# A 16-batch matmul with bias and residual on one core: joint waits and a joint store in SyncE's program, and the last store in two transfers by partitions

## The chip, the cores and the metric

The kernel runs on one core of one Trainium2 chip. The metric is device time in microseconds; the changed kernel is timed against the kernel before on the same chip. Before: 211.24 us, the median of three runs (211.44, 210.61, 211.24). The profile shows one execution more, of 211.06 us, whose span from the first to the last instruction is 208.7 us.

A core has a matrix engine (PE, its weight loads shown as PEld), VectorE (DVE), ScalarE (ACT), GpSimd (POOL) and SyncE (SP). Each follows its own list of instructions and waits on semaphores. Data moves between the large memory and the 128 partitions of the core's own memory through 16 transfer (DMA) engines. Here SP alone issues transfers.

## The reference

```python
def reference(x, weight, bias, residual):      # x: 16 x 512 x 1024, weight: 1024 x 768, all fp32
    return (np.matmul(x, weight) + bias + residual).astype(np.float32)
```

Flattened, x has 8,192 rows of 1,024 numbers; the residual and the output have 8,192 rows of 768.

## The kernel before

**Tiling.** The 8,192 rows form 8 groups of 1,024. In a group each of the 128 partitions holds 8 rows that follow one another in memory, so one group of x is 32 KB for each partition, one group of the residual or the output 24 KB. A row index j = 0 to 7 over all partitions is a subtile; there are 64 of them (`n_sub`).

**Buffers.** One large tensor `data` holds four places for residual groups (`r_home`, L97) and two for x groups (`x_half`, L94). Group g's residual lies in place g % 4, but that of group 7 (the last) lies in an x place. The weight is first loaded, as fp32, into residual place 3. Output is made in place: residual + product + bias, and is stored from there. So every load waits until what lay in its place has been used.

**Compute.** For each half of a group, ACT casts x to bf16 (`cast_x`, L112: two casts for a half, four for a group, each adding 1 to the semaphore `cast`), DVE and ACT transpose it in blocks, PE multiplies it by the weight into PSUM, DVE adds the product onto the residual (`evacuate`, L146, semaphore `ev`), and POOL adds the bias to two subtiles at a time (`add_bias`, L188, semaphore `add`). POOL also casts the weight at the start (L182, semaphore `wc`, which ends at `R` = 8). The last two subtiles get their bias ahead of the product, so for them DVE's `evacuate` comes last.

**SyncE's program.** The list `ORDER` (L16) names all transfers in the order in which SP issues them, and the loop at L216 makes waits and a transfer of each name:

- `x2a` is the first half (rows 0 to 3) of group 2's x, `x2b` the second. From group 2 on, part a waits until the first half of group g-2 has been cast, part b until both have (L227).
- `r3` is group 3's residual. It waits for `wc`, because the weight lay in its place; r7 waits for casts, r4 to r6 wait for a store from their place (L233 to L238).
- `load_into` (L208) makes a load wait for the one before it on the same semaphore: x parts a on `xa`, parts b on `xb`, residuals on `r`. So SP issues each next load of a kind only when the one before it has landed.
- `st5` is group 5's store; it waits for POOL's adds of the group's last subtiles. The stores from st3 on count on one semaphore, `st`. The last group's store is in three, by rows: `st7a` (0 to 3), `st7b` (4 and 5), `st7c` (6 and 7). st7c waits for DVE's last evacuation.
- At the end, SP waits until all stores from st3 on have landed (L253).

SP takes its list strictly in order: while it waits for one entry, all later ones are held up. All transfers go through one hardware queue and are worked off in about the order of issue. A transfer can carry one wait in its own instruction; a second wait is an instruction of its own (shown with L73).

Of the kernel before, what the change touches and what calls it, by code (L numbers as in the profile page):

```python
# [10 lines left out]
P = 128  # L11
Q = 32
G = 8
B = 4

ORDER = ("x0a w0 w1 bias x0b r0 x1a x1b r1 x2a x2b r2 x3a x3b r3 x4a x4b st0 st1 r4 x5a x5b r5 "  # L16
         "st2 x6a x6b r6 x7a x7b r7 st3 st4 st5 st6 st7a st7b st7c ").split()
PARTS = {"": (0, 8), "a": (0, 4), "b": (4, 8)}
LAST_PARTS = {"a": (0, 4), "b": (4, 6), "c": (6, 8)}


@with_exitstack
def kernel(
    ctx: ExitStack,
    tc: tile.TileContext,
    x: bass.AP,
    weight: bass.AP,
    bias: bass.AP,
    residual: bass.AP,
    out: bass.AP,  # L30
):
    nc = tc.nc
    with tc.tile_critical(name="all", no_gpsimd_drain=True), ExitStack() as es:  # L33
        emit(nc, es, x, weight, bias, residual, out)


def emit(nc, es, x, weight, bias, residual, out):
    x2d = x.flatten_outer_dims()
    res2d = residual.flatten_outer_dims()
    out2d = out.flatten_outer_dims()  # L40
    M, K = x2d.shape
    N = weight.shape[1]
    R = K // P
    KH = K // 2
    n_sub = M // P
    n_grp = n_sub // G
    n_bat = n_sub // B
    chunks = [(0, 512), (512, N - 512)]
    sp, act, dve, pool, pe = nc.sync, nc.scalar, nc.vector, nc.gpsimd, nc.tensor
# [4 lines left out]
    R_SLOT, X_SLOT = G * N, G * K  # L54
# [12 lines left out]
    def sem(name):  # L67
        if name not in sems:
            sems[name] = es.enter_context(nc.semaphore(name))
        return sems[name]  # L70

    def wait(eng, name, value):
        eng.wait_ge(sem(name), value)  # L73
# [14 lines left out]
    def group(ap, g):  # L88
        return ap[g * G * P:(g + 1) * G * P, :].rearrange("(p j) k -> p j k", p=P)

    def span(start, size):
        return data[:, start:start + size] if isinstance(start, int) else data[:, bass.ds(start, size)]

    def x_half(g, half):  # L94
        return span(X0 - (g % 2) * X_SLOT + half * (B * K), B * K).rearrange("p (t k) -> p t k", k=K)

    def r_home(g):  # L97

        return (g % 4) * R_SLOT + ((g + 1) // n_grp) * (X0 - 3 * R_SLOT)

    def r_rows(start, j, n):
        return span(start + j * N, n * N).rearrange("p (j n) -> p j n", n=N)
# [51 lines left out]
    cast, pt, res = Rising(dve, "cast", 1, 1), Rising(dve, "pt", 2, 2), Rising(dve, "r", 16, 16)  # L154
# [51 lines left out]
    landed, stored = {}, 0  # L206

    def load_into(name):  # L208

        before = landed.get(name, 0)  # L210
        landed[name] = before + 16
        if before:
            wait(sp, name, before)
        return name

    for name in ORDER:  # L216
        into = name
        if name == "bias":
            wait(sp, "ev", EV0)
            src, dst = bias[None, :].to_broadcast((P // Q, N)), bias_rows[0:P:Q, :]  # L220
        elif name[0] == "w":
            k0 = int(name[1]) * (R // 2)
            src, dst = w_rows[:, k0:k0 + R // 2, :], w_stage[:, k0:k0 + R // 2, :]
        elif name[0] == "x":
            g, part = int(name[1]), name[2:]
            j0, j1 = PARTS[part]
            if g > 1:  # L227
                wait(sp, "cast", 2 * (2 * g - 2 - (part == "a")))
            into = load_into(name[0] + part)
            src, dst = group(x2d, g)[:, j0:j1, :], x_half(g, j0 // B)  # L230
        elif name[0] == "r":
            g = int(name[1])
            if g == 3:  # L233
                wait(sp, "wc", R)
            elif g == n_grp - 1:
                wait(sp, "cast", 2 * (2 * g))
            elif g > 3:
                wait(sp, f"st{g - 4}", 16)  # L238
            into = load_into("r")
            src, dst = group(res2d, g), r_rows(r_home(g), 0, G)  # L240
        else:
            g = int(name[2])
            j0, j1 = (LAST_PARTS if g == n_grp - 1 else PARTS)[name[3:]]
            end = g * G + j1
            if end == n_sub:
                wait(sp, "ev", ev_end)
            else:
                wait(sp, "add", added[end - 1])
            src, dst = r_rows(r_home(g), j0, j1 - j0), group(out2d, g)[:, j0:j1, :]
            if g > 2:  # L250
                into, stored = "st", stored + 16
        sp.dma_start(out=dst, in_=src).then_inc(sem(into), 16)
    wait(sp, "st", stored)  # L253

# [2 lines left out]
    with pe.Fori(0, n_bat) as b:  # L257
        mv.wait()
        tm.wait()
        for i in range(B):  # L260
# [4 lines left out]
            for k in range(R):  # L265
                lhsT = words[:, k // 2, k % 2, :]
                for c, (n0, nl) in enumerate(chunks):
                    dst, rhs = po[:, i, n0:n0 + nl], w_sb[:, k, n0:n0 + nl]
                    if c == 0:
                        ins = pe.matmul(dst, lhsT=lhsT, rhs=rhs, start=(k == 0), stop=(k == R - 1))  # L270
                    else:
                        ins = pe.add_instruction(mybir.InstMatmult(  # L272
                            name=nc.get_next_instruction_name(),
# [34 lines left out]
```

## Time and profile before

| | us |
|---|---|
| median of three runs | 211.24 |
| the profiled execution | 211.06 |
| its span, first to last instruction | 208.7 |
| PE busy | 170.1 |
| DVE busy | 166.4 |
| ACT busy | 154.0 |
| POOL busy | 116.3 |

The shares of the span are 82, 80, 74 and 56%. The transfers move 87.05 MB, 61.88 MB read and 25.17 MB written, 417 GB/s over the span. The transfers that bear on the change, with the time from the issue by SP to the landing of the data:

| transfers | count | KB each | median us to landing |
|---|---|---|---|
| x halves | 16 | 2,048 | 17.0 |
| residual groups | 8 | 3,072 | 17.1 |
| stores of a group | 7 | 3,072 | 24.3 |
| st7a | 1 | 1,536 | 10.1 |
| st7b, st7c | 2 | 768 | 8.6 |

A transfer that takes 17 us to land has spent most of that in the queue: 2,048 KB at 417 GB/s are 5.0 us.

How to read the profile: a row of digits shows 40 equal slices of the span, each digit the busy share of a slice in tenths. In a table of windows each row has a stretch of the span, its length, the busy time of five engines with their instructions in brackets, the granted clock of the matrix engine (1.00 is full), the busy share of the 16 transfer engines and the GB/s that they moved. In a timeline, a row has the start, the time covered, the engine, the line and the operation; where several instructions are merged the count stands at the end.

### The profile page before, as it was taken

The page shows a single profiled execution, that of the slowest core. Times are in us where ns is not written, and L with a number is a line of the kernel's source. Part 1 is how long each engine was busy: PE and PEld are TensorE (multiplying, and loading weights), DVE is VectorE, ACT ScalarE, POOL GpSimd, SP SyncE. Part 2 cuts the span into 40 slices and gives each one's busy share as a digit, 9 for nine tenths or more (in the row PEclk, how much of TensorE's full clock was granted, in tenths as well). Part 3 has the DMA queues.
Part 4 walks back from the last instruction along what each step waited for, and adds up shares of the span by engine and source line. Part 5 has one row for each costly group of instructions (what it writes and reads, how often), then busy time and mean ns, then how long its engine had stood idle before and what let it go on. Part 6 is the DMA issues. An engine that isn't in the chain of part 4 may idle for free.

```text
span 208.7 us, 2850 instructions
## 1 busy us (share of the span) xinstructions
PE 170.1 (82%) x1024; PEld 50.4 (24%) x512; DVE 166.4 (80%) x180; ACT 154.0 (74%) x168; POOL 116.3 (56%) x44
## 2 busy tenths in 40 slices
PE   0000499999999999999999999999999999999700
PEld 0000122232333233223322333232223332322200
DVE  1009686899989998999899989998999899983400
ACT  0365998697989798979997998889897989720000
POOL 0066003918484757566665757484839392999600
PEclk9999999999999999999999999999999999999965
DMA  6999899999999999999999999999999999999993
GB/s 226 426 434 465 386 430 446 451 407 421 433 437 418 468 386 446 433 448 405 429 448 407 459 410 433 419 433 437 422 426 451 429 415 438 443 424 424 422 418 135
DMA packets 5192, 87.05 MB, mean 417 GB/s; under 512 B 580, under 2 KB 580, under 8 KB 840
## 3 DMA queue, kind: packets, MB, share of 16 engines
q1 hardware_dynamic: 5192, 87.05, 97.8%
HBM read 61.88 MB, written 25.17 MB: 417 GB/s over the span
## 4 chain that ended last, share of the span: by engine, by line
DVE 30%; ACT 22%; issue 16%; DMA 15%; PE 10%; ACTq 1%; DVEq 1%; SPq 0%
DVE xt L142 17%; DMA data<-in_x_dram 15%; ACT xt L119 12%; ACT xb L114 8%; DVE tq L136 7%; PE po L270 7%; DVE data L148 6%; PE po L272 3%; ACT L114 2%; DVEq L84 1%; ACTq L84 0%; ACTq L114 0%; ACTq L124 0%; DVEq L148 0%; SPq L303 0%
## 5 line engine op out<-in xcount | busy, mean ns | idle before, releaser
L270 PE MATMUL po<-w_sb,xt 128*128 128x512 bf16 x512 | 169.2, 383 | 27.0 <-DVE xt L142 24.0
L190 POOL TENSOR_TENSOR data<-data,bias_bc 128x1536 f32<-128x1536 f32 x32 | 109.9, 3453 | 68.5 <-DVE data L148 68.5
L272 PE MATMUL po<-w_sb,xt 128*128 128x256 bf16 x512 | 140.7, 275 | 0.0
L119 ACT COPY xt<-tq 32x512 uint32<-32x512 uint32 x128 | 79.0, 617 | 20.1 <-DVE tq L136 17.4
L142 DVE STREAM_TRANSPOSE xt<-xb 32x512 uint32<-32x512 uint32 x128 | 90.1, 704 | 2.7 <-ACT xb L114 0.7
L270 PEld LDWEIGHTS po<-w_sb,xt 128*128 x512 | 50.4, 98 | 146.2 <-issue 144.2
L148 DVE TENSOR_TENSOR data<-po,data 128x1536 f32 (+2 forms) x33 | 56.0, 1709 | 12.3 <-PE po L272 11.8
L114 ACT CAST xb<-data 128x2048 bf16 x32 | 64.9, 2077 | 0.3
L136 DVE STREAM_TRANSPOSE tq<-xb 128x1024 uint32<-128x1024 uint32 x16 | 19.8, 1235 | 1.6 <-ACT xb L114 1.6
L114 ACT ACT_TABLE_LOAD x8 | 10.3, 1283 | 9.6 <-DMA data<-in_x_dram 9.5
L185 POOL CAST w_sb<-data 128x768 bf16<-128x768 f32 x8 | 6.3, 826 | 12.1 <-DMA data<-in_weight_dram 12.1
L153 DVE LOAD_MASK_SELECT bias_bc<-bias_rows x1 | 0.0, 14 | 13.9 <-DMA bias_rows<-in_bias_dram 13.9
L150 DVE MEMSET bias_rows<- 128x768 f32 x1 | 0.7, 698 | 1.2 <-SPq L33 1.2
L153 DVE STREAM_SHUFFLE bias_bc<-bias_rows 128x768 f32<-128x768 f32 x1 | 1.0, 1021 | 0.0
L292 POOL MEMSET const-float32-0.0<- 128x1 f32 x1 | 0.1, 98 | 0.2 <-issue 0.2
L292 POOL MEMSET const-bfloat16-1.0<- 128x1 bf16 x1 | 0.1, 101 | 0.0
L292 POOL MEMSET const-uint8-127<- 128x1 uint8 x1 | 0.1, 101 | 0.0
L292 POOL MEMSET const-float32-1.0<- 128x1 f32 x1 | 0.1, 98 | 0.0
## 6 DMA issues: line engine op xcount, KB each, us to landing
data<-in_x_dram SPq DMA_DIRECT2D x16, 2048.0 KB, 17.0
data<-in_residual_dram SPq DMA_DIRECT2D x8, 3072.0 KB, 17.1
out_dram<-data SPq DMA_DIRECT2D x7, 3072.0 KB, 24.3
data<-in_weight_dram SPq DMA_DIRECT2D x2, 1536.0 KB, 12.2
out_dram<-data SPq DMA_DIRECT2D x1, 1536.0 KB, 10.1
out_dram<-data SPq DMA_DIRECT2D x2, 768.0 KB, 8.6
bias_rows<-in_bias_dram SPq DMA_DIRECT2D x1, 12.0 KB
```

The costliest lines, as they stand in the source:

```text
L84: self.eng.reg_add(self.reg, self.reg, self.step)
L114: act.copy(out=xb[:, c], in_=part.rearrange("p t (a j r) -> p t j a r", j=R // 2, r=2)).then_inc(sem("cast"), 1)
L119: act.copy(out=xt[q * Q:(q + 1) * Q, half, :, :, m * Q:(m + 1) * Q], in_=tq[m * Q:(m + 1) * Q, :, :, q]).then_inc(sem("mv"), 1)
L136: dve.transpose(out=tq[:], in_=xb_words(0)).then_inc(sem("tq"), 1)
L142: ins = dve.transpose(out=xt[q * Q:(q + 1) * Q, half, :, :, m * Q:(m + 1) * Q], in_=words[m * Q:(m + 1) * Q])
L148: dve.tensor_add(out=rt, in0=po[:, j % 4:j % 4 + n, :N], in1=rt).then_inc(sem("ev"), 1)
L150: dve.memset(bias_rows[:], 0.0).then_inc(sem("ev"), EV0)
L153: dve.stream_shuffle(out=bias_bc[:], in_=bias_rows[:], mask=[0] * 32).then_inc(sem("bb"), 1)
L185: pool.tensor_copy(out=w_sb[:, k, :], in_=w_stage[:, k, :]).then_inc(sem("wc"), 1)
L190: pool.tensor_add(out=rt, in0=rt, in1=bias_bc[:, None, :].to_broadcast((P, 2, N))).then_inc(sem("add"), 1)
L270: ins = pe.matmul(dst, lhsT=lhsT, rhs=rhs, start=(k == 0), stop=(k == R - 1))
L272: ins = pe.add_instruction(mybir.InstMatmult(name=nc.get_next_instruction_name(), ins=[pe.lower_ap(rhs), pe.lower_ap(lhsT, for_matmul_weig ...
```

## The change

It does four things, all in SP's list.

1. Joint waits of the x loads: part a waits until both halves of group g-2 have been cast, and part b has no wait on casts any more.
2. The wait on `wc` goes from r3 to x3a, two entries earlier in the list.
3. A joint store: st4 and st5 become one transfer, `st4+`, of two groups (6,144 KB), which waits for the adds of both.
4. The last entry, st7c, is issued as two transfers with the same wait: partitions 0 to 119, then partitions 120 to 127.

```diff
-         "st2 x6a x6b r6 x7a x7b r7 st3 st4 st5 st6 st7a st7b st7c ").split()
+         "st2 x6a x6b r6 x7a x7b r7 st3 st4+ st6 st7a st7b st7c ").split()
...
-            if g > 1:
-                wait(sp, "cast", 2 * (2 * g - 2 - (part == "a")))
+            if g > 1 and part == "a":
+                wait(sp, "cast", 2 * (2 * g - 2))
+            if g == 3 and part == "a":
+                wait(sp, "wc", R)
...
-            if g == 3:
-                wait(sp, "wc", R)
-            elif g == n_grp - 1:
+            if g == n_grp - 1:
                 wait(sp, "cast", 2 * (2 * g))
...
-            g = int(name[2])
-            j0, j1 = (LAST_PARTS if g == n_grp - 1 else PARTS)[name[3:]]
-            end = g * G + j1
+            g, part = int(name[2]), name[3:]
+            n = 2 if part == "+" else 1
+            j0, j1 = (LAST_PARTS if g == n_grp - 1 else PARTS)[part.strip("+")]
+            end = (g + n - 1) * G + j1
...
             src, dst = r_rows(r_home(g), j0, j1 - j0), group(out2d, g)[:, j0:j1, :]
+            if n > 1:
+                src = span(r_home(g), n * R_SLOT).rearrange("p (g k) -> p g k", g=n)
+                dst = out2d[g * G * P:(g + n) * G * P, :].rearrange(
+                    "(g p j) n -> p g (j n)", g=n, p=P)
             if g > 2:
                 into, stored = "st", stored + 16
+        if name == ORDER[-1]:
+            p0 = P - P // 16
+            sp.dma_start(out=dst[:p0], in_=src[:p0]).then_inc(sem(into), 16)
+            src, dst, stored = src[p0:], dst[p0:], stored + 16
         sp.dma_start(out=dst, in_=src).then_inc(sem(into), 16)
```

Groups 4 and 5 lie in residual places 0 and 1, side by side, so the joint store reads 48 KB in a row from each partition and writes two runs of 24 KB.

## The prediction

> **What bounds the kernel now.** I read the page's DMA part first, because the metric ends when the last store has landed, then SyncE's waits, then a fine table of the last microseconds.
>
> ```profile
> DMA  6999899999999999999999999999999999999993
> DMA packets 5192, 87.05 MB, mean 417 GB/s; under 512 B 580, under 2 KB 580, under 8 KB 840
> q1 hardware_dynamic: 5192, 87.05, 97.8%
> ```
>
> The transfer engines are full from the second slice to the last but one, 97.8% of 16 engines' span. The compute engines stand at 74 to 82%, and only a wait that empties the queue, or the manner in which it runs dry, can move the end.
>
> The packet counts tell how transfers spread. The 36 transfers over 128 partitions and the one of the bias over 4 partitions leave 580 packets under 512 B: 36 x 16 + 4. So I read one small closing packet for each engine used: 16 engines for 128 partitions, 4 for the bias. Between 512 B and 8 KB lie 840 - 580 = 260 packets: 4 of the bias and 256 of the last two stores, one of 6,144 B for each partition. Each engine thus has 8 packets of the last store.
>
> SyncE's waits (engine, line, what for: total us, times, longest) and its issues (start, us):
>
> ```profile
> SPq L73 <- DMA out_dram<-data: 9.0, 1, 9.0
> ```
> ```profile
> 198.10 0.34 SPq L252 DMA_DIRECT2D out_dram<-data  x1
> ```
>
> SyncE issues st7c at 198.10, has nothing left to do at 198.44 and waits 9.0 us, to 207.4. The other 1.3 us of the 208.7 are the closing handshakes. Now the end in slices of 0.2 us; the last two figures are the share of 16 engines and GB/s, and a packet counts where it starts:
>
> ```profile
> 204.60:204.80 0.20, 0.00 (x0) 0.00 (x0) 0.00 (x0) 0.00 (x0) 0.00 (x0) 0.50 0.95 399
> 204.80:205.00 0.20, 0.00 (x0) 0.00 (x0) 0.00 (x0) 0.00 (x0) 0.00 (x0) 0.50 0.74 307
> 205.00:205.20 0.20, 0.00 (x0) 0.00 (x0) 0.00 (x0) 0.00 (x0) 0.00 (x0) 0.50 0.46 184
> 205.20:205.40 0.20, 0.00 (x0) 0.00 (x0) 0.00 (x0) 0.00 (x0) 0.00 (x0) 0.50 0.09 31
> 205.40:205.60 0.20, 0.00 (x0) 0.00 (x0) 0.00 (x0) 0.00 (x0) 0.00 (x0) 0.50 0.08 31
> 205.60:205.80 0.20, 0.00 (x0) 0.00 (x0) 0.00 (x0) 0.00 (x0) 0.00 (x0) 0.50 0.00 0
> 205.80:206.00 0.20, 0.00 (x0) 0.00 (x0) 0.00 (x0) 0.00 (x0) 0.00 (x0) 0.50 0.07 31
> ...
> 206.60:206.80 0.20, 0.00 (x0) 0.00 (x0) 0.00 (x0) 0.00 (x0) 0.00 (x0) 0.50 0.07 31
> 206.80:207.00 0.20, 0.00 (x0) 0.00 (x0) 0.00 (x0) 0.00 (x0) 0.00 (x0) 0.50 0.00 0
> ```
>
> 31 GB/s in 0.2 us is 6.2 KB: one packet. From 205.2 on, exactly one packet starts at a time, seven of them in eight slices, 1.6 / 7 = 0.23 us each. Fifteen engines are done by about 205.2 + 0.23 = 205.4; one lags and ends about 207.0, eight packets (8 x 0.23 = 1.8 us, its whole share of st7c) after it had done st7b. So the last 1.5 us or so are one straggling engine, and this is what the change can reach. Which engine it is, no view tells.
>
> **The change, part by part.** *Joint waits.* The six loads x2b to x7b lose their cast wait, r3 loses the wait on wc, x3a gains it. A second wait is an instruction of its own:
>
> ```profile
> L73 SPq EVENT_SEMAPHORE  x17: 17/17/17, 32.7 to 152.9; - x17
> ```
>
> 17 - 6 - 1 + 1 = 11 remain, six less at 17 ns, 0.1 us in all. I cost it at nothing: SyncE waits many microseconds around each, and behind it the queue is full (an x load lands 17.0 us after its issue in the median, a residual 17.1). Were that backlog gone, it would be worth these 0.1 us.
>
> The price is that xNa now waits for all casts of group N-2, not for half of them. Where that bites follows from ScalarE's casts and SyncE's issues:
>
> ```profile
> 66.57 4.06 ACT L114 CAST xb<-data 128x2048 bf16 x2
> ```
> ```profile
> 66.97 5.22 SPq L252 DMA_DIRECT2D data<-in_x_dram  x2
> ```
>
> These casts are the 11th and 12th and end at 70.63. x4a, issued at 66.97, needs 12 in place of 10, so it goes out 3.7 us later, at about 70.7. Behind it on SyncE stands x4b, which waits for x3b's landing anyway until 71.8 and is issued at 71.87 as now; nothing else is late. Groups repeat every 21.4 us, so the 4th, 8th, 16th, 20th and 24th cast end near 27.8, 49.2, 92.0, 113.4 and 134.8, before x2a (32.81), x3a (49.89), x5a (96.68), x6a (116.06) and x7a (140.79) are issued today; x3a has only 0.7 us to spare. Between 66.97 and 70.7 the engines work off x3b (to 71.8) and r3 (issued 62.08, landing 17.0 us later), so 3.7 us out of some 8 us of backlog: nothing. Without that backlog it would cost its 3.7 us. wc has been complete since POOL's eight casts before 21 us, so x3a's new wait is free.
>
> *Joint store.* One issue of 0.43 us less; st4 goes out with st5 at 161.46 instead of at 157.11, 4.35 us later. Behind it in SyncE's order is only st6, which waits for its adds until 182.86 in any case. The queue at that time:
>
> ```profile
> out_dram<-data SPq DMA_DIRECT2D x3, 3072.0 KB, 28.0
> data<-in_residual_dram SPq DMA_DIRECT2D x1, 3072.0 KB, 13.8
> ```
>
> Stores issued here land after 28.0 us, so 4.35 us leave it far from dry, and r7 and st3 lie ahead: nothing, or 4.35 us if they did not. It still has one packet for each partition and group, and 16 closing packets less, which no row prices above noise.
>
> *The split.* One more issue, 0.34 us from 198.44 to 198.8, with more than 6 us of queue ahead of it: nothing; without that it would be 0.34 us. What counts is where packets go. No transfer of 120 or of 8 partitions is in the trace; the nearest rows are 128 partitions on 16 engines with 8 packets each, and 4 partitions on 4. Best end: 120 partitions on 15 engines, 8 packets each, at 0.23 us; the straggler is the one left out, and the 8 single packets go to engines that are done. Then the straggler ends near 207.0 - 1.8 = 205.2, the others at 205.4, and one packet of 0.23 us follows on eight of them: 205.65. Gain 207.0 - 205.65 = 1.3 us. If four of the 8 packets queue on one path, they take 0.9 us and the gain is 0.6 to 0.7 us, the near engines being done earlier. Worst end: the straggler is not left out, or the 15 run slower than the 16 (below). I take 1.2 us, close to the single packet, since the engines finish spread over 0.4 us and most of the extra packets fall into that. [...]
>
> *Sum.* 0 + 0 - 1.2 on the span of 208.7: 207.5. Around the span lie 211.06 - 208.7 = 2.4 us, which I leave; a shorter program could at most save some of these, and no row shows it. The profiled run takes 211.06, 0.18 under the median of 211.24, so 211.24 - 1.2 = 210.0.
>
> **Rivals.** *R1, two engines meet (slower).* With 128 partitions all 16 engines run at full pace (share 0.95 to 1.1 to the end). With 120 the assignment of partitions to engines may be another one, in which two engines read through the same part of the memory. Then 8 packets take 3.7 us instead of 1.8: the 15 engines end at 205.4 + 1.85 = 207.3, and with 0.23 to 0.9 us for the tail the transfers end at 207.5 to 208.2 instead of 207.0, 0.5 to 1.2 us later: 212.0 in the middle (211.7 to 212.4). If the straggler is among the fifteen as well, it ends at 207.0 + 1.85 + 0.23, and the time is 213.3. It decides from the point where 15 engines need more than 1.3 us extra, a pace under about 60%. For it: nothing but 128 partitions was ever run here at scale. Against: the bias shows four engines at work side by side, but with 3 KB each, too little to tell. [...]
>
> *R2, the straggler is among the fifteen.* It keeps its 8 packets and perhaps gets a ninth: 0 to +0.23 us, 211.2 to 211.5. For it: no view says which engine lags. Against: nothing either, save that one split leaves out exactly one.
>
> *R3, the lag is not where the trace puts it.* The lag of one engine may differ between executions; with 0.5 us of it in the typical one, the gain is 0.2 us: 211.0. Against: times before lie within 0.83 us of each other, and the profiled one in the middle.
>
> *R4, the shorter program counts.* Some of the 2.4 us outside the span go too: 209.2 with 0.8 of them. No row for it.
>
> **How the numbers follow.** Chances: forecast 0.44, R1 0.26 (of it 0.10 with the straggler among the fifteen), R2 0.15, R3 0.08, R4 0.07. The forecast's own range is 209.6 to 210.7 (straggler wholly gone, tail of four packets). The range 209.4 to 212.3 takes that, R2, R3 and most of R1's first part; out stay the 213.3 and most of R4, under 2 in 10. About what a measurement can tell from no change is 0.5%, 1.06 us: faster means under 210.18, slower over 212.3. Faster: three quarters of the forecast and R4, 0.33 + 0.07 = 0.40. Slower: 0.10 for the 213.3 and some 0.05 for the far end of R1's first part, 0.15. Same: 0.45.
>
> **What would show it.** Right: in the last 2 us no stretch of single packets at 31 GB/s, SyncE's last wait ends near 206.1, 256 packets under 8 KB for the last two stores again, but 580 - 16 - 16 + 15 + 8 = 571 small ones. x4a is issued near 70.7 and x4b near 71.9, the joint store at 161.5, and the DMA share stays at 9 tenths throughout. Wrong: a lone engine to the end (R2), or packets of the last store that take over 0.4 us on most engines (R1), or a hole in the DMA row near 70 or 160.

## The result, and the profile after

The changed kernel is slower by about 0.2%: 211.56 us median (20 runs, 210.89 to 211.97) against 211.09 us (20 runs, 210.61 to 211.50) on the same chip, ratio 1.002 with a 95% interval of 1.0011 to 1.0029, that is 0.23 to 0.61 us. The profiled execution takes 211.27 us with a span of 208.8.

The queue is as full as before. First the page's DMA part of the changed kernel:

```profile
DMA  6999999999999999999999999999999999999993
DMA packets 5183, 87.05 MB, mean 417 GB/s; under 512 B 571, under 2 KB 571, under 8 KB 831
q1 hardware_dynamic: 5183, 87.05, 97.8%
```

97.8% again, no hole. There are 571 closing packets: 34 transfers of 128 partitions with 16 each, 4 of the bias, and 15 + 8 = 23 for the two parts of the last store. So by the closing packets 120 partitions ran on 15 engines and 8 on eight. The other 831 - 571 = 260 packets under 8 KB are as before.

SyncE's program in the changed kernel (issues: start, time covered; then the row of its extra waits):

```profile
71.37 1.14 SPq L261 DMA_DIRECT2D data<-in_x_dram  x2
...
157.37 26.55 SPq L261 DMA_DIRECT2D out_dram<-data  x3
...
198.82 0.36 SPq L259 DMA_DIRECT2D out_dram<-data  x1
199.23 0.82 SPq L261 DMA_DIRECT2D out_dram<-data  x1
```
```profile
L73 SPq EVENT_SEMAPHORE  x10: 17/17/28, 33.2 to 152.8; - x10
```

x4a goes out at 71.37, x4b right behind it at 72.18; in the row of 157.37 the joint store stands between st3 and st6. Ten extra waits are left (two of x3a's are in one instruction, of 28 ns at 50.21). The two parts of the last store are issued at 198.82 and 199.23, more than four microseconds before their first packets start (from 203.08 on).

The end in slices of 0.2 us (last two figures: share of 16 engines, GB/s; a packet counts where it starts):

```profile
205.00:205.20 0.20, 0.00 (x0) 0.00 (x0) 0.00 (x0) 0.00 (x0) 0.00 (x0) 0.50 0.68 277
205.20:205.40 0.20, 0.00 (x0) 0.00 (x0) 0.00 (x0) 0.00 (x0) 0.00 (x0) 0.50 0.61 246
205.40:205.60 0.20, 0.00 (x0) 0.00 (x0) 0.00 (x0) 0.00 (x0) 0.00 (x0) 0.50 0.16 62
205.60:205.80 0.20, 0.00 (x0) 0.00 (x0) 0.00 (x0) 0.00 (x0) 0.00 (x0) 0.50 0.08 31
205.80:206.00 0.20, 0.00 (x0) 0.00 (x0) 0.00 (x0) 0.00 (x0) 0.00 (x0) 0.50 0.07 31
...
206.40:206.60 0.20, 0.00 (x0) 0.00 (x0) 0.00 (x0) 0.00 (x0) 0.00 (x0) 0.50 0.07 31
206.60:206.80 0.20, 0.00 (x0) 0.00 (x0) 0.00 (x0) 0.00 (x0) 0.00 (x0) 0.50 0.07 31
206.80:207.00 0.20, 0.00 (x0) 0.00 (x0) 0.00 (x0) 0.00 (x0) 0.00 (x0) 0.50 0.08 31
207.00:207.20 0.20, 0.00 (x0) 0.00 (x0) 0.00 (x0) 0.00 (x0) 0.00 (x0) 0.50 0.00 0
```

The lone engine is still there, one packet at a time from 205.6 on. There is now one in the slice from 206.8 too, where the kernel before has none. The packet rows of the stretch from 206.85 to 207.30 show what it is, first the kernel before, then the changed one:

```profile
DMA packets 1, 0.00 MB, mean 0 GB/s; under 512 B 1, under 2 KB 1, under 8 KB 1
```
```profile
DMA packets 3, 0.01 MB, mean 14 GB/s; under 512 B 2, under 2 KB 2, under 8 KB 3
```

The changed kernel has a closing packet, one packet of 6,144 B and a closing packet there: the lagging engine ends its eight packets of the wide part at 206.905, does one of the narrow part, and ends at 207.142. In the kernel before it closes once, at 206.958. The lagging engine was not left out; it got a ninth packet.

### The profile page after: what moved, and what is told of

It reads as the page before. It is cut to its first block, busy times and chain, and to the rows that moved or that the text cites. A ratio compares the mean times of both kernels' runs of the same rounds, so it can differ in the third digit from the quotient of the medians.

```text
span 208.8 us, 2843 instructions
## 1 busy us (share of the span) xinstructions
PE 170.7 (82%) x1024; PEld 50.6 (24%) x512; DVE 166.3 (80%) x180; ACT 154.0 (74%) x168; POOL 116.3 (56%) x44
## 3 DMA queue, kind: packets, MB, share of 16 engines
q1 hardware_dynamic: 5183, 87.05, 97.8%
## 4 chain that ended last, share of the span: by engine, by line
DVE 30%; ACT 22%; issue 16%; DMA 15%; PE 10%; ACTq 1%; DVEq 1%; SPq 0%
DVE xt L142 17%; DMA data<-in_x_dram 15%; ACT xt L119 12%; ACT xb L114 8%; DVE tq L136 7%; PE po L279 7%; DVE data L148 6%; PE po L281 3%; ACT L114 2%; DVEq L84 1%; ACTq L84 0%; ACTq L114 0%; ACTq L124 0%; DVEq L148 0%; SPq L312 0%
```

## The experiments

Four theories were on trial. **T1:** the lagging engine is among the first eight, and packets on it, at 0.23 us each, set the end. **T2:** the loss comes from SyncE's shorter program. **T3:** any further transfer at the end costs 0.2 us. **T4:** narrow transfers of neighbouring partitions hurt because engines meet on one part of the memory.

From run to run, 2.0 to 2.6 us lie around the span, and in the kernel before these vary more than the span does. So beside the ratio the table gives the difference of the mean spans of all runs, with twice its standard error, against the kernel before on the same chip; two kernels ran once, and for them the span stands alone.

| run | last store | packets on the lagging engine | ratio (95%) | span, us |
|---|---|---|---|---|
| e1 | 120 + 8 | 9 | 1.0011 (1.0002 to 1.0020) | +0.31 ± 0.10 |
| e2 | whole, shorter program | 8 | 1.0001 (0.9992 to 1.0009) | -0.03 ± 0.08 |
| e3 | 120 + 7 + 1 | 9 | 1.0023 (1.0012 to 1.0034) | +0.36 ± 0.08 |
| e4 | 112 + 16 | 8 | 1.0012 (1.0003 to 1.0020) | +0.23 ± 0.16 |
| f1 | ladder of nine parts | 9 | one run | 209.7 |
| f2 | 64 + 4 x 16 | 8 | 1.0012 (1.0001 to 1.0023) | +0.18 ± 0.10 |
| f3 | 96 + 4 x 8 | 10 | 1.0062 (1.0041 to 1.0083) | +1.31 ± 0.40 |
| g1 | 112 + 4 x 4, spread | 7 | 1.0005 (0.9997 to 1.0014) | -0.07 ± 0.09 |
| g2 | by rows, 2 x 128 | 8 (16 halves) | 0.9998 (0.9989 to 1.0007) | 0.00 ± 0.07 |
| h1 | whole, loop in SyncE | 8 | one run | 208.9 |
| p8 | whole, load of 8 behind | 9 | 1.0019 (1.0009 to 1.0028) | +0.29 ± 0.09 |
| p4 | whole, load of 4 behind | 8 | 1.0006 (0.9997 to 1.0015) | +0.02 ± 0.11 |
| q120 | 120 alone | 8 | 1.0009 (1.0000 to 1.0018) | -0.04 ± 0.12 |
| k1 | 96 + 4 x 8, spread | 10 | 1.0039 (1.0025 to 1.0053) | +0.77 ± 0.20 |

### The two halves of the change

**e1**, the split alone; e3 and e4 have the same lines with `[120, 7]` and `[112]`, f1 to f3 with longer lists:

```diff
+        if name == ORDER[-1]:
+            p0 = 0
+            for count in [120]:
+                sp.dma_start(out=dst[p0:p0 + count], in_=src[p0:p0 + count]).then_inc(sem(into), 16)
+                p0, stored = p0 + count, stored + 16
+            src, dst = src[p0:], dst[p0:]
         sp.dma_start(out=dst, in_=src).then_inc(sem(into), 16)
```

> The kernel before with only the last store split (partitions 0 to 119, then 120 to 127). T1 (the lagging engine is one of the first eight and gets a ninth packet of 6,144 B): the lone engine has nine packets at the end instead of eight, and the time is 0.2 to 0.4 us above before. T2 (the loss comes from SyncE's shorter program, the later x4a or the joint store): the split alone costs under 0.1 us.

**e2**, the change without the split:

```diff
-        if name == ORDER[-1]:
-            p0 = P - P // 16
-            sp.dma_start(out=dst[:p0], in_=src[:p0]).then_inc(sem(into), 16)
-            src, dst, stored = src[p0:], dst[p0:], stored + 16
```

> The changed kernel without the split: joint waits and joint store alone. T1: within 0.1 us of before, eight lone packets at the end. T2: 0.3 to 0.5 us above before.

The split alone costs 0.31 us of span, the shorter program nothing (-0.03 ± 0.08). T2 falls. In e1's trace the lone engine again has a closing packet, one packet and a closing packet after its eight.

### Which engine lags

**e3**, `[120, 7]` and the last partition:

> The kernel before with the last store in partitions 0 to 119, 120 to 126 and 127, so that the second part can use seven engines and the third one. T1a (the lagging engine is the eighth): it has eight packets at the end, no ninth, and the time is within 0.1 us of before. T1b (it is one of the first seven): it has nine (ten if the first) and the time is as with the split in two, 0.2 to 0.4 us above before, or 0.2 us more. T2: within 0.1 us of before in any case.

```profile
DMA packets 3, 0.01 MB, mean 18 GB/s; under 512 B 2, under 2 KB 2, under 8 KB 3
```

This is the packet row of e3 from 207.25 to 207.60, the end of the lone chain: still one extra packet between two closing ones, not two. So, if narrow parts take the engines in one fixed order, the lagging engine is not the eighth, nor the first.

**f1**, `[96, 7, 6, 5, 4, 3, 2, 1]` and a last four:

> The kernel before with the last store in nine parts of 96, 7, 6, 5, 4, 3, 2, 1 and 4 partitions. If a part of k partitions uses the first k engines, engine 1 to 7 and the rest have 14, 13, 12, 11, 9, 8, 7 and 6 packets, so the number of packets in the last chain of the lagging engine names it. T1a (the eighth): 6 packets. T1b: 7 to 14, and which number says which engine. If the parts go to engines in another way, the chain does not fit any of these numbers.

The stretch from 207.35 to 208.30 of f1, GB/s in 40 slices and the packets:

```profile
GB/s 0 0 259 0 0 0 0 0 0 0 0 0 259 0 0 0 0 0 0 0 0 0 259 0 0 0 0 0 0 0 0 0 0 0 0 0 0 0 0 0
DMA packets 7, 0.02 MB, mean 19 GB/s; under 512 B 4, under 2 KB 4, under 8 KB 7
```

Three single packets 0.24 us apart among four closing packets: the end of the wide part, then three narrow parts. Ahead of them the chain has the six packets of the wide part, each beginning where the one before ends and with no closing packet of its own between them. That makes nine, which by the list is the fifth engine if narrow parts take the engines in one fixed order, and it fits e3 (in the seven, not in the one) and the changed kernel (in the eight). The ladder ran once. Two of the six wide packets took 798 and 389 ns in place of 234, while other engines were at their narrow parts.

### Does a further transfer cost by itself?

**e4**, `[112]` and sixteen:

> The kernel before with the last store in partitions 0 to 111 and 112 to 127: 16 engines in both parts, seven packets and one. T1: every engine still has eight packets, so within 0.1 us of before. Rival T3 (a second transfer at the end costs time by itself, through its issue or its closing packet, whichever engines it uses): 0.2 to 0.4 us above before as with the split in 120 and 8.

**f2**, `[64, 16, 16, 16]` and sixteen:

> The kernel before with the last store in five parts of 64, 16, 16, 16 and 16 partitions: four transfers more, every engine still with eight packets. T1 (packets on the lagging engine count, at 0.23 us each): within 0.1 us of before, at most 15 ns for each closing packet on top. T3 (each further transfer at the end costs 0.2 us by itself): 0.8 us above before.

**f3**, `[96, 8, 8, 8]` and eight:

> The kernel before with the last store in five parts of 96, 8, 8, 8 and 8 partitions: as many transfers as in the five even parts, but ten packets on the first eight engines and six on the others. T1: two packets more on the lagging engine, 0.46 us above the five even parts. T3: the same as the five even parts, 0.8 us above before. If the lagging engine were among the last eight, 0.4 us less than the five even parts.

One further transfer (e4) and four (f2) cost the same, 0.2 us, so T3 falls in its plain form; but T1 alone gives them nothing. f3 is 1.31 us longer where T1 gives 0.46, and its spans scatter from 209.1 to 210.9. In the profiled runs of e4 and f2 the lagging engine's last eight packets take about the usual 0.23 us each (up to 0.25 in f2).

The traces tell more when all that lies ahead of the last group is left out. The lagging engine's closing packet of st6 comes more than 1.1 us behind all others', so it can be picked out in every trace. From there to its last closing packet pass 7.37 us with eight packets of one transfer (before: 199.593 to 206.958; the same in e2, h1, p4 and q120), 7.38 in e4, 7.46 in f2, and 7.64 to 7.65 with the ninth packet of the changed kernel, e1 and e3. So in e4's profile the split costs 0.02 us and in f2's 0.10. The rest of what they are longer lay ahead of the split: the lagging engine closed st6 at 199.739 and 199.692 there. These are single executions; why the mean spans of e4 and f2 are 0.2 us longer stays open.

**g2**, the split by rows:

```diff
+        if name == ORDER[-1]:
+            sp.dma_start(out=dst[:, :1], in_=src[:, :1]).then_inc(sem(into), 16)
+            src, dst, stored = src[:, 1:], dst[:, 1:], stored + 16
```

> The kernel before with the last store in two by rows, row 6 and row 7 of all 128 partitions, sixteen packets of 3,072 B on every engine. One transfer more, nothing moved between engines, no narrow transfer. T3: span 0.2 us longer than before. T4 and T1: within 0.1 us of before.

0.00 ± 0.07: a further transfer over all partitions cost nothing.

**g1**, an attempt to relieve the fifth engine:

```diff
+        if name == ORDER[-1]:
+            sp.dma_start(out=dst[:112], in_=src[:112]).then_inc(sem(into), 16)
+            for p0 in (112, 113, 114):
+                sp.dma_start(out=dst[p0:P:4], in_=src[p0:P:4]).then_inc(sem(into), 16)
+            src, dst, stored = src[115:P:4], dst[115:P:4], stored + 64
```

> The kernel before with the last store in five parts: partitions 0 to 111, then 112, 116, 120, 124, then 113 and so on in steps of four, four partitions in each. The lagging engine, the fifth, has seven packets instead of eight, the first four have eleven, on different parts of the memory. T1 (packets on the lagging engine set the end): seven packets in its last chain, and the span 0.2 us shorter than before. T3 (any further transfer costs 0.2 us): no change, the gain and the cost together. T4 (small transfers collide in the memory): no collision here, so as T1.

The profiled execution has seven packets in the lone chain, which closes at 206.812 (206.958 before), 7.15 us after its closing packet of st6 in place of 7.37: one packet less, as T1 has it. But over 12 runs the span is 0.07 ± 0.09 shorter, less than the 0.2 expected: not to be told from no change, and no version to keep.

### The ninth packet alone

**p8** and **p4** (with 4 in place of 8): the last store is left whole, and a load follows it.

```diff
+    wait(sp, "cast", 4 * n_grp)
+    sp.dma_start(out=data[P - 8:, X1:X1 + 2 * N], in_=res2d[:2 * 8, :].rearrange(
+        "(p j) n -> p (j n)", j=2)).then_inc(sem("st"), 16)
-    wait(sp, "st", stored)
+    wait(sp, "st", stored + 16)
```

> The kernel before with one more transfer behind the last store: a load of 6,144 B into each of partitions 120 to 127, into a place that is free by then. The last store stays whole. T1: the lagging engine gets a ninth packet and the span grows by 0.23 us. T4 alone (the narrow store hurts because its packets meet others in the memory, not by the ninth packet): under 0.1 us.

> The same with partitions 124 to 127 alone, so that only the first four engines get a packet more and the lagging fifth none. T1: within 0.1 us of before. If any narrow transfer at the end costs time: 0.2 us.

The ends of the lone chains, p8 from 207.10 to 207.50, then p4 from 207.05 to 207.50:

```profile
DMA packets 3, 0.01 MB, mean 15 GB/s; under 512 B 2, under 2 KB 2, under 8 KB 3
```
```profile
DMA packets 1, 0.00 MB, mean 0 GB/s; under 512 B 1, under 2 KB 1, under 8 KB 1
```

Eight partitions, with the ninth packet on the lagging engine: +0.29 ± 0.09. Four partitions, without it: +0.02 ± 0.11, although this too is a narrow transfer at the very end. From st6's closing packet to the last, p8 takes 7.61 us and p4 7.37. This is T1 by itself.

**q120**, the wide part by itself:

```diff
+        if name == ORDER[-1]:
+            src, dst = src[:P - P // 16], dst[:P - P // 16]
```

> The kernel before with the last store for partitions 0 to 119 alone; rows 6 and 7 of the last group of partitions 120 to 127 are not stored. The lagging engine has eight packets as before, one engine none. T1: within 0.1 us of before. T4b (a wide store of other than 128 partitions spreads over the engines in another way and slows the lagging one): 0.1 to 0.2 us above before.

-0.04 ± 0.12: the end comes no later with the wide part on 15 engines, and leaving out an engine that does not lag gained nothing. The 15 do not run quite as evenly as the 16: in this trace five packets of 6,144 B take 273 to 446 ns, where in the kernel before none takes over 238. The next-to-last engine ends at 206.13 and the lagging one at 207.20, so this costs nothing here.

**k1**, f3 with the eights spread in steps of four partitions:

```diff
+        if name == ORDER[-1]:
+            sp.dma_start(out=dst[:96], in_=src[:96]).then_inc(sem(into), 16)
+            for p0 in (96, 97, 98):
+                sp.dma_start(out=dst[p0:P:4], in_=src[p0:P:4]).then_inc(sem(into), 16)
+            src, dst, stored = src[99:P:4], dst[99:P:4], stored + 64
```

> Like the first-eight kernel (96 partitions, then four times eight), but the eights are partitions 96, 100 to 124 and so on in steps of four. The lagging engine has ten packets. T1: 0.46 us above before. T4 (the 1.3 us of the contiguous eights came from four engines at a time on one part of the memory): the spread eights lose that, so 0.4 to 0.7 us above before. If it came from the transfers as such: 1.3 us again.

+0.77 ± 0.20 in five runs, against +1.31 ± 0.40 with neighbouring partitions. That is a little over the 0.4 to 0.7 of T4 and well over the 0.46 of T1. The two intervals overlap slightly, so the means lean to T4 and do not settle it. The traces do not support it: from st6's closing packet to the last, the lagging engine takes 0.52 us more than before in f3 (one of its shorter executions, and about what T1 gives) and 0.92 in k1, and packets of up to 576 ns occur with the spread eights too. q120 has slow packets with no narrow transfer at all. What makes packets slow when a store is split by partitions stays open.

### Why the engine lags

A store of 128 partitions raises its semaphore 16 times (112 raises for the seven stores that count on `st`), which I read as once for each engine. By these times in the trace of before, the last raise is behind the fifteenth by 0.04 us at x4b (88.9), 0.30 at r4 (111.1), 0.6 from x6a (140.7) to r7 (170.0), and 1.61 at st6 (200.1): it falls back by 0.17 to 0.33 us in each group store from st3 to st6 and kept its 0.6 us through the loads from x6a to r7. From 169.4 us on, 31 packets of 24,576 B, one behind the other, take 925 to 964 ns in before, and every other takes 912; in the changed kernel 32 take 926 to 964. In before the compute engines end at 198.07, and the engine's last packet of that size, from 198.69 on, takes 912 ns; in the changed kernel they end at 198.79, and the last starts at 198.58 and takes 926. The smaller ones behind it are as quick as the others' (460 and 234 ns): in before the engine closes st6 1.53 us behind the next one, and the last store 1.54.

**h1** adds work for SyncE while st3 is under way:

```diff
+        if name == "st6":
+            with sp.Fori(0, 50):
+                wait(sp, "bias", 16)
+                wait(sp, "wc", R)
```

> The kernel before with a loop of 50 rounds of two satisfied waits in SyncE's program ahead of st6, while st3 to st5 are in the queue: one engine's work, some hundred short instructions more in about 15 us. If the lag of the one engine comes from the recording or the fetching of instructions, it grows by clearly more than 0.3 us for a store in that stretch. If it belongs to the stores alone, it stays at 0.25 to 0.35 us for each.

The loop ran until 177.3, which covers st3. There the lag grows by 0.43 us, against 0.24 in before and 0.20 to 0.30 in the other traces; in st4, after the loop, by 0.33 as in before. In this one run, then, a loop of instructions that touch no data came with 0.19 us more lag in one store; whether it caused it, and by what, is open.

## Why the prediction was wrong

- **What bounds the kernel.** Right: a full queue, and at its end one engine alone for some 1.5 us.
- **Joint waits.** Right, with e2: nothing. x4a was the one load to go out later, at 71.37 (70.7 forecast; the casts end at 71.35 in this execution, 0.7 us later than before), x4b right behind it.
- **Joint store.** Right, nothing: issued at 162.18, no hole.
- **The split.** Here it failed, in the sentence "the straggler is the one left out". The wide part did go to 15 engines with eight packets each, near full pace, as assumed (six of the last store's packets take 269 to 429 ns, the others 234), and the narrow part to eight engines. But by e3 and f1 the lagging engine is the fifth, in both parts. The gain of 1.2 us became a loss of one packet: 0.23 us by the price of the prediction, 0.29 ± 0.09 in p8, 0.31 ± 0.10 in e1. The second issue took 0.82 us and not 0.34, hidden by the queue ahead of it, as the prediction has it. I had said that no view tells which engine lags, and still gave the best end the largest chance; with nothing to go by, one engine in sixteen is left out, and the forecast's 0.44 had no row behind it. That 120 partitions take 15 engines and 8 take eight was the prediction's estimate, beside rows of 128 on 16 and 4 on 4; no run before it shows such a transfer, and the 15 + 8 closing packets among the changed kernel's 571 bear it out.
- **R2** is what happened, with its mechanism and nearly its price (0 to +0.23 us; the whole change cost 0.42 us with an interval of 0.23 to 0.61). That the measured 211.56 lies inside 209.4 to 212.3 is due to R2 and R1, for which the range was widened, and not to the forecast.
- **R1** falls as a price: q120 is -0.04 ± 0.12, and all engines but the lagging one are done by 206.13, far ahead of R1's 207.3. That two engines on one part of the memory take twice as long (3.7 us in place of 1.8) was the prediction's supposition, and no run shows it; q120's five slow packets of up to 446 ns and f1's of 798 may be packets that meet, but no trace shows where.
- **R3 and R4.** The lag varies, 1.2 to 1.8 us between the last two closing packets of st6 in the 16 traces, but never vanishes. Nothing was saved around the span: e2's time there is 2.09 us in the mean, 2.11 before.

What stays open: why the means of 112 + 16 and 64 + 4 x 16 are 0.2 us longer with eight packets on the lagging engine, when their traces show 0.02 and 0.10 us of it behind st6, and so whether the last tenth of the change's loss is the packet or the narrowness.

## What to carry to other kernels

When the transfers end with one engine alone, find out which engine it is before moving work off "the last one": here a ladder of narrow transfers, each for one partition less, named it by the number of packets in its chain (nine in f1, so the fifth). The narrow transfers fit one order of the engines: with eight or seven partitions the lagging engine got a ninth packet (p8, e3), with four it got none (eight packets in p4, seven in g1). Leaving out an engine that doesn't lag gained nothing (q120, -0.04 ± 0.12).

## What the runs showed of the hardware that was not expected

- One engine of 16, the fifth by the ladder, falls back in the group stores from st3 to st6, by 13 to 52 ns for 31 packets of 24,576 B in before (925 to 964 ns against 912), and not in the loads from x6a to r7 (0.6 us behind throughout) nor from 198.69 us on, after the end of the compute engines at 198.07; in one run, a loop of empty waits came with a lag that grew by 0.43 us in one store, against 0.24.
- When the last store is split by partitions, single packets of 6,144 B took 798 (f1) or 822 ns (f3) in place of 234, and a split into neighbouring eights scattered the span over 1.8 us (f3). A store of 120 partitions alone shows a few such packets as well (up to 446 ns, q120), one split by rows none (g2).
- The second of the two transfers issued back to back at the end takes SyncE 0.70 us (e3) to 1.08 us (f2), 0.82 in the changed kernel, where a transfer issued alone takes 0.33.
